# A gated DeltaNet stage whose matrix engine order is written by the program

## The chip, the cores and the metric

One core of one Trainium2 chip runs the kernel. The metric is device time in microseconds (us) from one run of the whole kernel. The instruction streams are PE (TensorE matmul), with PEld for its weight loads, DVE (VectorE), ACT (ScalarE), POOL (GpSimd), and SP, which issues all DMA transfers from one queue of instructions. Each engine starts its instructions in the order of its own stream.

## The reference

One inference step of a two-layer trunk for 512 prompt tokens and 8 sample tokens (T = 520), model width 1024, all in f32:

```python
for i in range(2):
    x = x + (gdn_mixer, dsw_mixer)[i](rmsnorm(x))
    x = x + square(relu(rmsnorm(x) @ w_up)) @ w_down
# gdn_mixer: 8 q/k heads of 128, 16 value heads of 128
proj = x @ w_in                               # q | k | v | z | b | a
q, k, v = silu(causal_conv4(proj[:3]))        # q, k: L2 norm per head
t_inv = inverse(I + strict(beta * (k @ k.T) * decay))     # per chunk
v_new = t_inv @ (v * beta) - t_inv @ (k * beta * exp(gc)) @ S
o = (q * exp(gc)) @ S + ((q @ k.T) * decay) @ v_new
S = S * exp(gc_last) + (k * exp(gc_last - gc)).T @ v_new  # next chunk
out = (rmsnorm(o) * silu(z)) @ w_out
```

The sample tokens take one step of the same recurrence, each from its own stored state S0 (16 heads of 8 x 128 x 128). The mixer of the second layer is a windowed attention. The change is inside the first mixer.

## The kernel before

The stages follow one another: gdn, mlp0, dsw, mlp1. Every product with a weight is made of three reduced-precision products (lines L165 to L167; a weight tile `raw` is split on ACT into `whi` and on DVE into `wlo`; tiles `mm` hold the results, 260 tokens at a time). One weight tile of 128 columns is 48 such matmuls.

The gdn stage works on eight pairs p = 0..7: one q/k head and its two value heads, in four chunks of 128 tokens, so eight units of 128 x 128 a pair. For each pair:

- `key`, `query`, `values`: projections, convolution, SiLU; PE transposes (`kqt`, `vtr`).
- `decay`: the DMA `ET <- Dg` (L595) brings cumulated log-decays over all partitions; DVE subtracts (L596), ACT takes absolute value and exponential (L597, L598); PE makes `kk` (L611) and DVE makes `E` from `kk` and `ET` (L603).
- `invert`: the 32 x 32 diagonal blocks of `E` go to DRAM (tile `D1`, L629) and come back spread over the partitions (`Ft`, L632); POOL substitutes in 31 steps of a multiply and an add (L638, L641; the buffer is a part of the tile `held`); the result goes to DRAM (`D2`, L642) and comes back as `Uf`, also a part of `held` (L646).
- `attend` (L618, POOL L619) turns `ET` into the attention matrix; `merge` (L653 to L683) joins inverted blocks by DVE transposes and small matmuls (`px`, `pu`).
- `scan`: for each chunk in turn the products `pk` (with the state `S`), `pv`, `pS` and `po`, with DVE, ACT and PE taking turns (`R` L712, `S` L724, `osb` L738 and L739).
- `sample`: loads the two `S0` tiles (L792, in `states`), products `sks` (L816), a transpose `sut` (L826), and the updated state by ACT and POOL (L837, L838) back to DRAM (L839).
- `gates`, `out`: the z projection; DVE scales `osb` (L862), PE transposes it (`otr`, L867), DVE gates it, and the split operands `onh` and `onl` go into the output projection, whose results DVE adds to x (L892).

A scheduler orders each engine's stream from the program order and priorities: the functions marked `urgent` get a priority of 2000. `states` of a pair stands at the pair's head in the program, ahead of `invert` of the next pair, and its DMAs keep program order:

```python
for p in range(QK_HEADS):
    A = pairs[p]
    A.states()
    A.values()
    if p < last:
        pairs[p + 1].key()
        pairs[p + 1].decay()
        pairs[p + 1].invert()
```

Of the kernel before, what the change touches and what calls it, by code (L numbers as in the profile page):

```python
# [38 lines left out]

KEEP = 104  # L40
# [9 lines left out]

class Common:
# [10 lines left out]
        # what lives as long as the kernel: the residual stream and constants, and the split operand  # L62
# [25 lines left out]
    def kept_rows(self):  # L88
        """The cached rows that stay in the sample's k/v buffers, a piece of them at each step."""
# [44 lines left out]
    def weights(self, cols, nk=KT):  # L134
        """cols: DRAM [nk * 128, n] pieces; gives each 128 columns in parts for the products."""
# [21 lines left out]
    def proj(self, w, mov, evac, m=P, halves=(0, 1)):  # L157
        nc = self.nc
        nk = len(mov)
        for hf in halves:  # L160
# [7 lines left out]
            evac(ps[:m], hf, s)  # L168
# [4 lines left out]
    def split_x(self, gain, k, hf, x=None):  # L173
        """The moving operand of the next projection, x * gain, as a rule not normalized yet."""
        nc = self.nc
        x = self.x if x is None else x
        s = slice(hf * H, hf * H + H)
        nc.scalar.activation(self.xh[:, k, s], x[:, k, s], AF.Copy, scale=gain[:, k : k + 1])  # L178
        nc.vector.scalar_tensor_tensor(  # L179
            self.xl[:, k, s], x[:, k, s], gain[:, k : k + 1], self.xh[:, k, s].bitcast(F32), ALU.mult, ALU.subtract  # L180
        )
# [14 lines left out]
    def mean_sq(self, acc):  # L196
        """1 / (mean square + eps) by token: [128, 5], the last column for the sample tokens."""
# [13 lines left out]
    def rsqrt(self, pool, x, eng, tag):  # L211
        """1 / sqrt(x) for positive x [128, n], by Newton's iteration from an estimate made of its bits."""
# [12 lines left out]
    def bcast(self, pool, r, tag="bc"):  # L225
        """A figure by token, [128, 5], over all partitions: [128, T]."""
# [21 lines left out]
    # the tensor engine's clock goes up with use: let it run while the rows come in  # L248
# [94 lines left out]
# before the scan of pair p: the output projection of some pairs, from one tile of x to another  # L343
OUTP = {p: [((p - 2,), 0, 8)] for p in range(2, 8)}
OUTP[8] = [((6,), 0, 8), ((7,), 0, 8)]
EARLY = (7,)
# [9 lines left out]
def gdn(K, l, rms, gain, done):  # L356
    """Gated DeltaNet, one pair of value heads (those of one q/k head) after the other, in chunks
    of 128 tokens. The first projections go without 1 / rms, which their result gets; meanwhile
    the moving operand is normalized for the rest."""
# [6 lines left out]
    with ExitStack() as ctx:  # L366
# [3 lines left out]
        xn = cp.tile([P, KT * T], F32, name="xn").rearrange("p (k t) -> p k t", k=KT)  # L370
        for k in range(KT):
            nc.gpsimd.tensor_tensor(xn[:, k], K.x[:, k], rb, ALU.mult)
# [19 lines left out]
        # eyeU[q4 * 32 + r, m, j] = (j == 4 * m + q4)  # L392
# [4 lines left out]
        # ---- beta and the log-decay, token-major  # L397
# [8 lines left out]
        # silu(x) = x/2 (1 + tanh(x/2)): the halves go to the weights, exactly  # L406
# [4 lines left out]
        # ---- the sample group's convolution history, feature-major: hist[p, f, b * 3 + j]  # L411
# [47 lines left out]
        # cumulated in each chunk; gc, its last, and their exponentials  # L459
# [7 lines left out]
        # gc as rows, in DRAM: a pair reads its own over all partitions  # L467
# [9 lines left out]
        # the sample tokens' beta and exp(g), over all partitions: [128, 2, 16, 8]  # L477
# [17 lines left out]
        # ---- buffers whose zero parts are set once  # L495
# [4 lines left out]
        def row(name):  # L500
            return K.tile(gp, [P, T], F32, tag="row", name=name, bufs=8)

        raw = []

        def project(w, ft, dest=None):
# [12 lines left out]
            if len(raw) < RAW:  # L518
# [3 lines left out]
                if len(raw) == RAW:  # L522
                    for hf in range(2):
                        for k in range(KT):
                            K.split_x(gain, k, hf, xn)
# [870 lines left out]
```

## Time and profile before

| | |
|---|---|
| median of 3 runs | 2165.23 us (2164.26 to 2168.29) |
| profiled execution, span | 2168.5 us |
| gdn stage in it, from the span's start | about 806 us |
| mlp0, dsw, mlp1 | about 1362 us |
| PE busy, whole span | 1989.6 us (92%) |
| PE busy in the first 806 us | 655.12 us |
| granted PE clock, first 806 us and rest | 0.87 and 1.00 |

The span is the profiled execution's time; it lies 3.3 us over the median of the three runs. The stage boundary is where the first activity of the MLP (L322) appears, at 807.8 us, with the last addition of L892 at 804.9 us. A PE that is busy at a granted clock of 0.87 does 0.87 of the work that it would do at full clock, so busy time times granted clock is the work of a stretch at full clock.

### The profile page before, as it was taken

Reading aid. Unit: us, or ns where it says so; the run is one execution under the profiler, and the core shown is the slowest. Engines: PE = TensorE matmul, PEld = TensorE weight load, DVE = VectorE, ACT = ScalarE, POOL = GpSimd, SP = SyncE. Lnnn points to the kernel's source line nnn. Section 1 sums busy time; section 2 is a strip of 40 time slices with the busy share of each in tenths; the row PEclk is TensorE's granted clock in tenths of the full one; section 3 lists DMA queues with packets and bytes.
Section 4 is the critical chain, followed back from the end, with each engine's and each line's share of the span. In section 5 each row is a group of like instructions: output and inputs, shape, how many; then the busy total and the mean of one; then the engine's idle time right before and its main releaser. Section 6 shows DMA issues by size and latency. Waiting matters only on the chain. (4 is left out here: it accounts for less than half of the span.)

```text
span 2168.5 us, 41683 instructions
## 1 busy us (share of the span) xinstructions
PE 1989.6 (92%) x16361; PEld 1950.9 (90%) x16361; DVE 1349.5 (62%) x3332; ACT 899.4 (41%) x2416; POOL 535.6 (25%) x821
## 2 busy tenths in 40 slices
PE   7677889896969789999999999999999989999999
PEld 6677778896969679999999999999999989999998
DVE  6754856785766584544556467676766785544544
ACT  5434444444334353223244555555555444233231
POOL 4253264355253230000002133232332250000000
PEclk8889989988979889999999999999999999999999
DMA  5334554764655538666676675534445343333332
GB/s 145 68 71 114 149 157 127 223 181 128 204 150 158 168 96 303 228 238 242 232 248 227 221 242 141 140 108 123 120 128 137 97 115 88 89 98 89 94 92 79
DMA packets 416277, 328.54 MB, mean 152 GB/s; under 512 B 48408, under 2 KB 404568, under 8 KB 413896
## 3 DMA queue, kind: packets, MB, share of 16 engines
q1 hardware_dynamic: 416080, 325.88, 50.4%
q8 instruction: 128, 2.10, 0.4%
q14 instruction: 69, 0.57, 0.1%
HBM read 302.19 MB, written 132.83 MB: 201 GB/s over the span
## 5 line engine op out<-in xcount | busy, mean ns | idle before, releaser
L165 PE MATMUL mm<-split,whi 128*128 128x260 f32 (+1 forms) x2960 | 866.7, 293 | 3.8 <-ACT split L178 2.5
L167 PE MATMUL mm<-split,wlo 128*128 128x260 f32 (+1 forms) x2960 | 851.8, 288 | 9.4 <-DVE wlo L132 9.4
L166 PE MATMUL mm<-split,whi 128*128 128x260 f32 (+1 forms) x2960 | 851.8, 288 | 8.7 <-DVE split L179 8.6
L166 PEld LDWEIGHTS mm<-split,whi 128*128 128x128 f32 (+1 forms) x2960 | 567.1, 192 | 12.3 <-DVE split L179 10.5
L167 PEld LDWEIGHTS mm<-split,wlo 128*128 128x128 f32 (+1 forms) x2960 | 566.5, 191 | 11.8 <-DVE wlo L132 10.9
L165 PEld LDWEIGHTS mm<-split,whi 128*128 128x128 f32 (+1 forms) x2960 | 567.6, 192 | 7.2 <-ACT split L178 3.7
L132 DVE TENSOR_TENSOR wlo<-raw,whi 128x1024 fp32r<-128x1024 f32 (+1 forms) x273 | 341.0, 1249 | 195.3 <-ACT whi L131 177.7
L131 ACT CAST whi<-raw 128x1024 fp32r<-128x1024 f32 (+1 forms) x273 | 285.8, 1047 | 411.7 <-PE mm L166 396.1
L167 PE MATMUL mm<-hh,wlo 128*128 128x260 f32 x1024 | 288.8, 282 | 0.0
L166 PE MATMUL mm<-hl,whi 128*128 128x260 f32 x1024 | 288.8, 282 | 0.0
L165 PE MATMUL mm<-hh,whi 128*128 128x260 f32 x1024 | 288.1, 283 | 0.0
L167 PEld LDWEIGHTS mm<-hh,wlo 128*128 128x128 f32 x1024 | 193.0, 188 | 0.0
L166 PEld LDWEIGHTS mm<-hl,whi 128*128 128x128 f32 x1024 | 192.8, 188 | 0.0
L165 PEld LDWEIGHTS mm<-hh,whi 128*128 128x128 f32 x1024 | 192.3, 188 | 0.0
L335 DVE TENSOR_TENSOR t<-mm,bc 128x260 f32<-128x260 f32 x128 | 54.8, 428 | 153.0 <-PE mm L167 153.0
L191 POOL TENSOR_TENSOR acc<-acc,sq 128x260 f32<-128x260 f32 x42 | 37.8, 909 | 382.0 <-ACT sq L190 381.3
L638 POOL TENSOR_TENSOR fs<-Ft,held 128x60 f32<-128x60 f32 (+24 forms) x248 | 100.5, 405 | 89.2 <-DMA Ft<-D 58.7
L131 ACT CAST hh<-q 128x260 fp32r<-128x260 f32 x128 | 52.5, 410 | 122.1 <-DVE q L322 122.1
L165 PE MATMUL mm<-onh,whi 128*128 128x260 f32 x256 | 90.3, 356 | 13.0 <-DVE base L892 7.9
L530 DVE SCALAR_TENSOR_TENSOR conv<-pre,held,conv 128x512 f32<-128x512 f32 x96 | 77.6, 808 | 30.1 <-POOL pre L508 27.2
L641 POOL TENSOR_TENSOR held<-held,fs 128x60 f32<-128x60 f32 (+24 forms) x248 | 90.5, 365 | 18.5
L132 DVE TENSOR_TENSOR hl<-q,hh 128x260 fp32r<-128x260 f32 x128 | 54.9, 429 | 57.0 <-ACT hh L131 57.0
(374 smaller groups left out, 3319.4 us busy)
## 6 DMA issues: line engine op xcount, KB each, us to landing
out_dram<-in_cache_kv_w_dram SPq DMA_DIRECT2D x112, 832.0 KB
raw<-in_dsw_w_in_dram SPq DMA_DIRECT2D x72, 512.0 KB
raw<-in_mlp_w_up_dram SPq DMA_DIRECT2D x64, 512.0 KB
raw<-in_mlp_w_down_dram SPq DMA_DIRECT2D x64, 512.0 KB
raw<-in_gdn_w_in_dram SPq DMA_DIRECT2D x48, 512.0 KB
S<-in_state_gdn_dram SPq DMA_DIRECT2D x16, 512.0 KB
raw<-in_gdn_w_out_dram SPq DMA_DIRECT2D x16, 512.0 KB
ub<-Du SPq DMA_DIRECT2D x16, 512.0 KB
```

Source lines behind the costliest of these rows:

```text
L131: nc.scalar.copy(hi, src)
L132: nc.vector.tensor_tensor(lo, src, hi.bitcast(F32), ALU.subtract)
L165: nc.tensor.matmul(ps[:m], lhsT=w[0][:, k, :m], rhs=xh[:, s], start=k == 0, stop=False)
L166: nc.tensor.matmul(ps[:m], lhsT=w[0][:, k, :m], rhs=xl[:, s], start=False, stop=False)
L167: nc.tensor.matmul(ps[:m], lhsT=w[1][:, k, :m], rhs=xh[:, s], start=False, stop=k == nk - 1)
L191: nc.gpsimd.tensor_tensor(acc[:, s], acc[:, s], t, ALU.add)
L335: nc.vector.tensor_tensor(t, ps, r2[:, s], ALU.mult)
L530: nc.vector.scalar_tensor_tensor(a, pre[:, j : j + NP], convw[:, ft, j : j + 1], a, ALU.mult, ALU.add)
L638: nc.gpsimd.tensor_tensor(tmp[:, :m, :n], Ft[:, None, j + 1 :, j].to_broadcast([P, m, n]), Uo[:, :m, j : j + 1].to_broadcast([P, m, n]), A ...
L641: nc.gpsimd.tensor_tensor(Uo[:, :m, j + 1 :], Uo[:, :m, j + 1 :], tmp[:, :m, :n], ALU.add)
```

## The change

In the gdn stage the scheduler no longer orders PE: the program does (`manual_schedule` for PE alone; DVE, ACT, POOL and SP are still ordered by the scheduler). The string `ORDER` lists the projections: K, Q, V, Z of each pair, and O for the output projection, for pairs 0 and 1, 2 and 3, 4 and 5 in one product each, then 6, then 7. A projection is a generator that yields after each three matmuls; the pair's other steps (`key_chain`, `query_chain`, `value_chain`, `scan`, `sample`, `out`) are generators too, launched with a model wait and stepped between those threes by `Weave`. The first ready item of the list is taken; K and Q of pair p want scan p - 3 emitted, V scan p - 2, Z out p - 2. Other edits:

- `gap` (the DMA `ET <- Dg`, the subtraction and the exponentials) is emitted at the start of `key_chain`, once scan p - 2 is emitted.
- `states` is called when the sample chain starts (after query p and sample p - 1), and `S0` has 2 buffers in place of 4.
- `kd` (two DVE products a pair, L555) is gone. ACT copies `kt`, and scales `vd` in each chunk; `pS` is one product of 256 columns in place of two of 128.
- `E` has 3 buffers in place of 2, and `osb`, `X1`, `X2`, `T2` become parts of `E`; `R` and `vn` have 1 buffer in place of 2, the rows of the projections 6 in place of 8.
- The clearing of `pre` goes from POOL to DVE. The normalised x of the later projections, made by POOL in eight products, is made after the sixth projection in row buffers, and no longer ahead of the stage.

```diff
+class Weave:
+    def __init__(self):
+        self.t, self.chains, self.done = 0.0, [], set()
+    def launch(self, steps, name, after=0.0):
+        self.chains.append([self.t + after, steps, name])
+    def pump(self):
+        for c in list(self.chains):
+            while c in self.chains and c[0] <= self.t:
+                self.step(c)
+    def step(self, c):
+        took, wait = next(c[1], (0.0, None))
+        self.t += took
+        if wait is None:
+            self.chains.remove(c)
...
+    def dense(self, steps):
+        for took in steps:
+            self.t += took
+            self.pump()
...
+                if k == nk - 1:
+                    evac(ps[:m], hf, s)
+                yield 3 * MMT
...
+ORDER = "K0 Q0 V0 K1 Q1 Z0 K2 Q2 V1 Z1 K3 Q3 V2 O01 Z2 K4 Q4 V3 Z3 K5 Q5 V4 O23 Z4 K6 Q6 V5 Z5 K7 Q7 V6 Z6 V7 Z7 O45 O6 O7"
+CONV_T, INV_T, SCAN_T, OUT_T, LOAD_T = 8.0, 60.0, (2.2, 2.2, 2.2), 5.0, 8.0
...
+            nc.vector.memset(pre[:, 0:3], 0.0)
...
+                    for k in range(KT):
+                        xn = row("xn")
+                        nc.gpsimd.tensor_tensor(xn, K.x[:, k], rb, ALU.mult)
+                        for hf in range(2):
...
-                kd = self.kd = K.tile(gp, [P, C4, 2, P], F32, tag="kd", name="kd", bufs=2)
-                for v in range(2):
-                    nc.vector.tensor_tensor(kd[:, :, v], pst, egc[:, 2, :, 2 * p + v, None].to_broadcast([P, C4, P]), ALU.mult)
+                kt = self.kt = K.tile(gp, [P, C4, P], F32, tag="kt", name="kt", bufs=2)
+                nc.scalar.copy(kt, pst)
                 nc.vector.tensor_scalar(ss, ss, EPS, None, ALU.add)
...
+                if p > 1:
+                    yield from W.until(f"scan{p - 2}")
+                self.gap()
...
+                yield 0.5, 2.0
+                with tc.high_priority(PRIO):
+                    self.decay()
+                    self.invert()
+                yield 4 * FULL, INV_T
+                yield from self.merge()
...
+                ET = self.ET = K.tile(gp, [P, U, P], F32, tag="ET", name="ET", bufs=2)
+                E4 = ET.rearrange("p (c v) d -> p c v d", v=2)
+                nc.sync.dma_start(E4, Dg[None, :, hh, :].to_broadcast([P, C4, 2, P]))
+                nc.vector.tensor_tensor(E4, E4, gc[:, :, hh, None].to_broadcast([P, C4, 2, P]), ALU.subtract)
+                nc.scalar.activation(ET, ET, AF.Abs)
+                nc.scalar.activation(ET, ET, AF.Exp, scale=-1.0)
...
+                E = self.E = K.tile(gp, [P, U, P], F32, tag="E", name="E", bufs=3)
...
+                W.launch(self.scan(), f"scan{p}")
+                W.launch(self.sample(), f"sample{p}", CONV_T)
...
+                osb = self.osb = self.E
...
+                            nc.scalar.activation(vd[:, v], pv[:, v * P : (v + 1) * P], AF.Copy, scale=egc[:, 2, c, 2 * p + v : 2 * p + v + 1])
+                        vn = K.tile(gp, [P, 2, P], F32, tag="vn", name="vn", bufs=1)
+                        nc.scalar.copy(vn.rearrange("p v d -> p (v d)"), pv[:, :256])
...
+                        nc.tensor.matmul(pS[:, :256], lhsT=self.kt[:, c], rhs=vd.rearrange("p v d -> p (v d)"), start=True, stop=True)
...
+                            W.launch(self.out(i, c0, c1), f"out{p}.{i}" if c1 < C4 else f"out{p}", 6 * FULL + 2.0)
+                    yield 6 * FULL, SCAN_T[2]
...
-                    S0 = K.tile(gp, [P, NS, P], F32, tag="S0", name="S0", bufs=4)
+                    S0 = K.tile(gp, [P, NS, P], F32, tag="S0", name="S0", bufs=2)
...
+                yield from W.until(f"query{p}", *([f"sample{p - 1}"] if p else []))
+                self.states()
...
+                yield 0.0, LOAD_T
...
+                yield from W.until(f"gates{p}", f"sample{p}", *([f"out{p}.{i - 1}"] if i else []))
...
+                yield 0.0, OUT_T
...
+        def waits(name, p):
+            if name == "O":
+                return [f"out{q}" for q in p if q < last] + [f"out{last}.1"] * (last in p)
+            n, of = dict(K=(3, "scan"), Q=(3, "scan"), V=(2, "scan"), Z=(2, "out"))[name]
...
+        with tc.manual_schedule(engines={mybir.EngineType.PE}):
+            while todo:
+                ready = [x for x in todo if W.done.issuperset(waits(*x)) and (x[0] != "Q" or ("K", x[1]) not in todo)]
+                if not ready:
+                    W.need(*waits(*todo[0]))
+                    continue
+                todo.remove(ready[0])
+                name, p = ready[0]
+                A = pairs[p[0]]
+                W.dense(out_proj(p, 0, KT) if name == "O" else {"K": A.key, "Q": A.query, "V": A.values, "Z": A.gates}[name]())
+            assert not W.chains, W.chains
```

How it moves instructions. First place: SP around the `S0` loads of pair 2 (tiles 2630 and 2632 before, 3111 and 3113 after) and the inversion of pair 3 (`D1`, `Ft`, `D2`). `raw` are weight loads, `out_9` and `out_10` cache rows copied through, `Du` the sample's u. Before, the stream of SP reads:

```order
L792 DMA S0_2630<-in_state_gdn_dram 128x8x128
L146 DMA raw_4486<-in_gdn_w_in_dram 128x8x128
L98 DMA out_9_dram<-in_cache_kv_w128_dram 16x2944
L792 DMA S0_2632<-in_state_gdn_dram 128x8x128
L629 DMA D1_2911<-E_2892 32x8x32 x4
L146 DMA raw_4493<-in_gdn_w_in_dram 128x8x128
L98 DMA out_9_dram<-in_cache_kv_w128_dram 16x13312
L632 DMA Ft_2917<-D1_2911 128x1x1024
```

After, the same place reads:

```order
L702 DMA D1_3008<-E_2994 32x8x32 x4
L705 DMA Ft_3014<-D1_3008 128x1x1024
L190 DMA raw_3587<-in_gdn_w_out_dram 128x4x256
L142 DMA out_9_dram<-in_cache_kv_w128_dram 16x13312
L190 DMA raw_3668<-in_gdn_w_in_dram 128x8x128
L142 DMA out_9_dram<-in_cache_kv_w128_dram 16x2944
L715 DMA D2_3009<-held_261 4x256x32
L719 DMA held_261<-D2_3009 32x8x32
L895 DMA S0_3111<-in_state_gdn_dram 128x8x128
L895 DMA S0_3113<-in_state_gdn_dram 128x8x128
```

The loads stood ahead of `D1` of pair 3, and now stand behind its `D2`. The same holds for pair 4 (behind `D2` of pair 5); pair 7's loads stand behind `D2` of pair 7 and behind the stores of pair 6's states. Those of the other pairs stand behind no `D2` of a later pair.

Second place: SP, the `ET` load of a pair and the `D2` store of another inversion. Before, `ET` of pair 4 stands ahead of `D2` of pair 3:

```order
L146 DMA raw_4745<-in_gdn_w_in_dram 128x8x128
L98 DMA out_10_dram<-in_cache_kv_w512_dram 16x13312
L595 DMA ET_3945<-Dg_429 128x4x256
L747 DMA out_2_dram<-S_3419 128x2x128
L146 DMA raw_4893<-in_gdn_w_in_dram 128x8x128
L98 DMA out_10_dram<-in_cache_kv_w512_dram 16x13312
L642 DMA D2_2912<-held_270 4x256x32
```

After, `ET` of pair 3 stands behind `D2` of pair 2 (`raw` are weight loads, `out_2` the final state of a scan):

```order
L715 DMA D2_2364<-held_261 4x256x32
L635 DMA ET_2920<-Dg_420 128x4x256
L190 DMA raw_3496<-in_gdn_w_out_dram 128x4x256
L719 DMA held_261<-D2_2364 32x8x32 x3
L850 DMA out_2_dram<-S_2884 128x2x128
```

From pair 2 on, each `ET` load now stands behind the `D2` store of the pair before; before, those of pairs 3, 4, 5 and 7 stood ahead of it.

Third place: PE, the transposes `otr` of pair 1's output, the `kk` of pair 3 and the `sks` of pair 2. Before, `otr` stands 122 rows behind the last `po` of its scan:

```order
L165 MATMUL mm_3772<-split_70,whi_3694 128x260
L166 MATMUL mm_3772<-split_70,whi_3694 128x260
L167 MATMUL mm_3772<-split_70,wlo_3695 128x260
L165 MATMUL mm_3772<-split_70,whi_3694 128x260
L166 MATMUL mm_3772<-split_70,whi_3694 128x260
L867 MATMUL otr_2605<-base_69,osb_2284 128x128 x4
L867 MATMUL otr_2614<-base_69,osb_2284 128x128 x4
```

After, it stands 43 rows behind it, right after `kk` of pair 3:

```order
L685 MATMUL kk_2995<-kq_2277 128x128 x4
L663 MATMUL kqt_3085<-base_69,kq_2277 128x128 x4
L685 MATMUL kk_3098<-kq_2277 128x128 x4
L782 MATMUL vtr_3105<-base_69,conv_2852 128x128 x4
L214 MATMUL mm_2978<-split_70,whi_2861 128x260
L215 MATMUL mm_2978<-split_70,whi_2861 128x260
L216 MATMUL mm_2978<-split_70,wlo_2862 128x260
L982 MATMUL otr_3132<-base_69,E_1238 128x128 x4
L982 MATMUL otr_3140<-base_69,E_1238 128x128 x4
L214 MATMUL mm_2978<-split_70,whi_2861 128x260
L215 MATMUL mm_2978<-split_70,whi_2861 128x260
L216 MATMUL mm_2978<-split_70,wlo_2862 128x260
```

From this `kk` to the first `sks` of pair 2 there are 60 projection matmuls and 21 others in all (rows of equal products taken apart), and from the last `po` of scan 1 (ahead of them) 93 and 33. Before, `sks` of pair 2 stands some 180 rows behind `kk` of pair 3.

Fourth place: DVE around the scaling of a pair's output (L862 before, L975 after; `osb` is now `E`) and the subtraction in `ET` for the pair two later. Before, the last rows ahead of the scaling of pair 1's output are these (wide `base` rows are steps of a Newton iteration); the subtraction for pair 3 stands some 30 rows earlier:

```order
L758 SCALAR_TENSOR_TENSOR sz_3448<-zt_3558,mm_3533 128x260
L783 COPY base_69<-sst_3092 128x16
L785 COPY base_69<-sst_3092 128x8
L222 SCALAR_TENSOR_TENSOR base_69<-base_69 128x24
L220 TENSOR_TENSOR base_69<-base_69 128x24
L221 TENSOR_TENSOR base_69<-base_69 128x24
L222 SCALAR_TENSOR_TENSOR base_69<-base_69 128x24
L220 TENSOR_TENSOR base_69<-base_69 128x24
L221 TENSOR_TENSOR base_69<-base_69 128x24
L222 SCALAR_TENSOR_TENSOR base_69<-base_69 128x24
L862 TENSOR_TENSOR osb_2284<-osb_2284,base_69 128x1024
```

After, for pair 5's output (`E_5036`) with the subtraction for pair 7:

```order
L636 TENSOR_TENSOR ET_7020<-ET_7020,held_261 128x1024
L271 TENSOR_TENSOR base_69<-base_69 128x4
L272 TENSOR_TENSOR base_69<-base_69 128x24
L272 TENSOR_TENSOR base_69<-base_69 128x4
L273 SCALAR_TENSOR_TENSOR base_69<-base_69 128x24
L273 SCALAR_TENSOR_TENSOR base_69<-base_69 128x4
L975 TENSOR_TENSOR E_5036<-E_5036,base_69 128x1024
```

In both, the subtraction stands ahead of the scaling. After, `E` of the pair two later (L676) stands behind it again, 9 rows further here.

More of the change, by code (lines that the diff above doesn't have):

```diff
@@ L38, in urgent @@
     return g
+MMT, FULL = 0.12, 0.225
 KEEP = 104
@@ L48, with need, until @@
 PACE = dict(gdn=1, mlp0=1, dsw=1, mlp1=1)
+class Weave:
[12 more added lines that the diff above has]
+            self.chains.remove(c)
+            self.done.add(c[2])
+        else:
+            c[0] = max(c[0], self.t) + max(wait, 0.05)
+    def dense(self, steps):
+        for took in steps:
+            self.t += took
+            self.pump()
+    def need(self, *names):
+        while not self.done.issuperset(names):
+            c = min(self.chains, key=lambda c: c[0])
+            self.t = max(self.t, c[0])
+            self.step(c)
+    def until(self, *names):
+        while not self.done.issuperset(names):
+            yield 0.0, 0.3
 class Common:
@@ L157, in proj, with proj_steps @@
     def proj(self, w, mov, evac, m=P, halves=(0, 1)):
+        for _ in self.proj_steps(w, mov, evac, m, halves):
+            pass
+    def proj_steps(self, w, mov, evac, m=P, halves=(0, 1)):
         nc = self.nc
@@ L515, in ev @@
                     nc.scalar.copy(news[:, ft, :], ps[:, H - NS :])
-            K.proj(w, mov, ev)
+            yield from K.proj_steps(w, mov, ev)
             if len(raw) < RAW:
@@ L532, in project @@
             nc.scalar.activation(t, a, AF.Tanh)
-            dest = a if dest is None else dest
-            nc.vector.scalar_tensor_tensor(dest, t, 1.0, a, ALU.add, ALU.mult)
-            return dest
+            if not out:
+                out.append(a)
+            nc.vector.scalar_tensor_tensor(out[0], t, 1.0, a, ALU.add, ALU.mult)
         class Pair:
@@ new lines, in merge @@
+                yield 1.7, 2.0
+                with tc.high_priority(PRIO):
+                    pus = {o: K.bank("pu", t).rearrange("p (u j) -> p u j", j=32) for o, t in ((0, "misc"), (64, "misc"))}
+                    for o in (0, 64):
+                        for u in range(U):
+                            t0 = T64[0:32, u, 0:32] if o == 0 else T2[:, u]
+                            nc.tensor.matmul(pus[o][o : o + 32, u], lhsT=t0, rhs=X1[o][:, u], start=True, stop=True)
+                        nc.scalar.copy(Uf[o : o + 32, :, o + 32 : o + 64], pus[o][o : o + 32, :U])
+                    for u in range(U):
+                        nc.tensor.matmul(pus[0][32:64, u], lhsT=X1[0][:, u], rhs=T64[0:32, u, 0:32], start=True, stop=True)
+                    nc.scalar.copy(T64[32:64, :, 0:32], pus[0][32:64, :U])
@@ new lines, in merge @@
+                yield 1.7, 2.5
+                with tc.high_priority(PRIO):
+                    px = K.bank("px2")
+                    pxt = px.rearrange("p (u j) -> p u j", j=64)
+                    for u in range(U):
+                        nc.tensor.matmul(pxt[0:64, u], lhsT=E[64:128, u, 0:64], rhs=Uf[64:128, u, 64:128], start=True, stop=True)
+                    nc.scalar.copy(X2, pxt[0:64])
+                yield 1.0, 2.0
+                with tc.high_priority(PRIO):
+                    pu = K.bank("pu2")
+                    put = pu.rearrange("p (u j) -> p u j", j=64)
+                    for u in range(U):
+                        nc.tensor.matmul(put[0:64, u], lhsT=T64[:, u], rhs=X2[:, u], start=True, stop=True)
+                    nc.scalar.copy(Uf[0:64, :, 64:128], put[0:64])
@@ L698, in scan @@
             def scan(self):
-                p, hh, kq, vt, col, Uf = self.p, self.hh, self.kq, self.vt, self.col, self.Uf
+                p = self.p
+                yield from W.until(*([f"scan{p - 1}"] if p else []), f"key{p}", f"query{p}", f"value{p}.0", f"value{p}.1")
+                hh, kq, vt, col, Uf = self.hh, self.kq, self.vt, self.col, self.Uf
                 S = None
-                oss = self.oss
-                osb = self.osb = K.tile(gp, [P, U, P], F32, tag="osb", name="osb")
+                oss, cuts = self.oss, LASTC if p == last else ((0, C4),)
@@ L742, in scan @@
-                    for v in range(2):
-                        u = 2 * c + v
-                        junk = K.tile(gp, [P, P], F32, tag="junk", name="junk", bufs=2)
-                        nc.scalar.activation(junk, osb[:, u], AF.Square, accum_out=oss[:, u : u + 1])
+                        with tc.high_priority(PRIO):
+                            Sf = S.rearrange("p v d -> p (v d)")
+                            pk = K.bank("pk", "scan", 256)
+                            nc.tensor.matmul(pk[:, :256], lhsT=kq[:, 0, cs], rhs=Sf, start=True, stop=True)
+                            r = K.tile(gp, [P, 2, P], F32, tag="R", name="R", bufs=1)
+                            for v in range(2):
+                                nc.vector.scalar_tensor_tensor(r[:, v], pk[:, v * P : (v + 1) * P], col[:, 2, c, v : v + 1], vt[:, c, v], ALU.mult, ALU.add)
@@ L888, in out_proj @@
                     for halves in ((0,), (1,)) if end else ((0, 1),):
+                        if halves == (1,):
+                            W.need(f"out{last}")
                         for k, w in ws:
@@ L894, in ev @@
                                     done(k, hf)
-                            K.proj(w, [m for p in ps for m in omov[p]], ev, halves=halves)
+                            yield from K.proj_steps(w, [m for p in ps for m in omov[p]], ev, halves=halves)
                     ws = []
```

273 lines of the change are left out of this document (116 added, 157 removed).

## The prediction

> **What bounds the kernel now.** I read the page's head, then the stretches of time before and after the end of the gdn stage, to see what the rest of the kernel can contribute.
>
> ```profile
> span 2168.5 us, 41683 instructions
> 0.00:806.00 806.00, 655.12 (x5267) 626.80 (x5268) 546.02 (x1546) 339.21 (x977) 329.69 (x662) 0.87 0.51 144
> 806.00:2168.00 1362.00, 1334.48 (x11097) 1324.14 (x11095) 803.48 (x1787) 560.22 (x1440) 205.92 (x159) 1.00 0.51 156
> 20.00:240.00 220.00, 164.22 (x1330) 154.84 (x1328) 145.90 (x405) 92.86 (x253) 85.46 (x181) 0.87 0.37 92
> 240.00:806.00 566.00, 475.74 (x3847) 457.81 (x3848) 393.73 (x1117) 234.11 (x700) 237.86 (x461) 0.87 0.56 161
> 774.00:806.00 32.00, 21.82 (x147) 20.09 (x146) 30.95 (x88) 18.18 (x51) 15.57 (x16) 0.84 0.34 102
> 850.00:950.00 100.00, 100.00 (x838) 100.00 (x837) 14.90 (x35) 6.49 (x17) 1.00 0.69 239
> ```
>
> The columns are the stretch, its length, busy time (and instructions) of PE, PEld, DVE, ACT, POOL, then PE's granted clock. After 806 us PE is full at clock 1.00, and the change does not touch that part. In the stage no engine is full: DVE is busy 546 of 806 us, PE 655. PE's work there at full clock is busy time times clock: 164.22 x 0.87 = 143 us in 20 to 240, and 475.74 x 0.87 = 414 in 240 to 806. So 77 us are lost in the first stretch and 566 - 414 = 152 in the second, to idleness and to the slow clock together. The second stretch starts where scan 1 starts. At full clock one projection matmul takes 100/838 = 0.119 us. What PE waits for, and what the SP queue waits for, in 20 to 806:
>
> ```profile
> PE sut L826 <- DVE base L819: 34.5, 5, 13.2
> PE px L660 <- DMA held<-D: 21.4, 3, 11.3
> PE pv L715 <- DVE R L712: 13.7, 4, 8.9
> SPq L642 <- POOL held L526: 37.9, 2, 19.6
> SPq L642 <- POOL held L641: 37.6, 4, 15.0
> SPq L146 <- DVE wlo L132: 111.1, 16, 18.3
> ```
>
> So no single wait bounds the stage: PE's losses are chains of small latencies, the longest the inversion. The SP rows matter most for what follows: SP stands still at the `D2` store (L642) until POOL has finished. One pair's inversion in order of time:
>
> ```profile
> 409.56 2.15 DVE L603 SCALAR_TENSOR_TENSOR E<-kk,base,ET 128x128 f32<-128x128 f32 x8
> 411.74 1.81 SPq L629 DMA_DIRECT2D D<-E  x4
> 428.28 1.21 POOL L638 TENSOR_TENSOR fs<-Ft,held 128x31 f32<-128x31 f32 x1 [7.33 <-DMA Ft<-D]
> 456.22 0.61 SPq L642 DMA_DIRECT2D D<-held  x1
> ```
>
> From the end of `E` (411.7) to the `D2` store there are 44.5 us.
>
> **The change, part by part.** The work of PE hardly changes: `pS` streams the same 256 columns. I therefore keep 414 us for the second stretch and 77 us lost for the first, and put the whole change into one question: how much is lost after scan 1's start, against 152 us.
>
> *Gain.* The new order has 309 to 417 projection matmuls (37 to 50 us) and 60 to 133 small ones between a pair's `kk` and its `px`. So the wait on the inversion, and those inside scans that other work now separates, have cover: all of the 152 us is up for removal, except what follows.
>
> *Sample states (S0).* The price of a load is in these rows: the first `sks` starts 5.7 us after its load is issued, and waits for it.
>
> ```profile
> 747.55 2.21 SPq L792 DMA_DIRECT2D S<-in_state_gdn_dram  x2
> 753.25 1.95 PE L816 MATMUL sks<-base,S 128*128 128x2 f32 x16 [1.57 <-DMA S<-in_state_gdn_dram]
> ```
>
> For pairs 2 and 4 the loads now stand behind `D2` of the next pair's inversion, so they issue no earlier than 44.5 us after that pair's `E`, and arrive at about 50. PE reaches `sks` 60 projection matmuls and 21 small ones after `kk`: 60 x 0.119 = 7.2 us, and some 2.5 us at the rate of the eight `kk` in the row of the next fence, so 10 us. PE's order is fixed, so nothing passes the waiting `sks`. Pair 7 waits likewise on its own inversion, but reaches `sks` 303 projection matmuls (36 us) and 89 others after `kk`, about 50 us; with the stores of pair 6 ahead in the queue I take 10 us, between 0 and 20.
>
> *ET and the output transposes.* `ET` is loaded only after the last `po` of scan p - 2, as before; the question is what PE does meanwhile.
>
> ```profile
> 437.27 0.37 SPq L595 DMA_DIRECT2D ET<-Dg  x1
> 446.52 1.26 DVE L596 TENSOR_TENSOR ET<-ET,held 128x1024 f32<-128x1024 f32 x1 [4.47 <-DMA ET<-Dg]
> 437.03 1.06 PE L735 MATMUL po<-S,kq 128*128 128x256 f32 x2
> 458.30 2.61 DVE L862 TENSOR_TENSOR osb<-osb,base 128x1024 f32<-128x1024 f32 x1
> 461.35 0.82 PE L867 MATMUL otr<-base,osb 128*128 128x128 f32 x6
> 409.95 1.05 PE L611 MATMUL kk<-kq 128*128 128x128 f32 x8
> ```
>
> Before, `otr` runs 24 us after the last `po`, with other work between. Now PE is there after 6 to 9 us, while DVE has the subtraction, then rows of the Newton iteration and of convolutions, then the scaling ahead of it. From the last `po`: 0.2 to issue, 9.25 to land, 1.26 to subtract, 2 to 9 for the rows between (about 0.17 us a small one and 0.8 us a convolution step, by their counts for each pair), 1.2 to 2.6 to scale. That is 14 to 20 us, and PE waits 9, 12, 10, 5 and 6 us for the outputs of pairs 0, 2, 3, 4 and 5. Pair 1 is worse: `ET` of pair 3 stands behind `D2` of pair 2. `E` of pair 2 ends some 21 us after scan 0, `D2` issues 44.5 later, at 65; PE is through scan 1 after 35 us of work (198 projection matmuls, 24 us, and 51 others, mostly the scan's larger products), the wait of 9 and some slow clock, at 48. `ET` is thus 17 us late and `otr` ready 38 us after the last `po`: a wait of 29.
>
> With these the `sks` waits follow. Pair 4: `E` of pair 5 at 21 after scan 3, loads arrive at 21 + 44.5 + 5.7 = 71; PE has done 18 (84 projection matmuls, 10 us, and 81 others) and waited 10, and waits 43 more. Pair 2: `E` of pair 3 at 42, loads arrive at 92; PE is there at 15 + 29 = 44, and waits 48. Sum of `sks` 48 + 43 + 10 = 101 (bounds 70 and 120: the bare 44.5 + 5.7 less 15, twice, and all of it), sum of `otr` 71 (bounds 36, with six waits of 6 us if DVE's rows between are done early, and 95).
>
> *Slow clock.* A hole is followed by a slow stretch:
>
> ```profile
> 181.90:191.10 9.20, 0.30 (x4) 0.09 (x2) 1.74 (x5) 0.00 (x0) 0.56 (x4) 0.75 0.26 47
> 191.10:210.00 18.90, 18.90 (x135) 18.80 (x136) 8.58 (x19) 8.47 (x24) 1.01 (x2) 0.85 0.54 178
> 530.50:542.10 11.60, 0.32 (x5) 0.14 (x3) 3.71 (x12) 4.08 (x9) 0.00 (x0) 0.68 0.56 72
> 542.10:560.00 17.90, 17.90 (x174) 16.88 (x175) 13.51 (x35) 4.08 (x11) 4.91 (x2) 0.73 0.33 109
> ```
>
> The 18.9 us after the first lose 0.15 x 18.9 = 2.8 us, the 17.9 after the second 0.27 x 17.9 = 4.8. Nine waits (six `otr`, three `sks`) at 3.8 make 34, between 25 and 43. The Trainium skill ("TensorE: Matmul & The Clock Gate", Part 1: The HAM clock gate) says that an idle window of about 3.4 us halves the rate and about 3.4 us of busy time restores it; the trace agrees on the fall and shows a longer recovery. By the page a hole would cost 1.7 us, nine 15, and the estimate would come out 19 us lower; I go by the rows.
>
> *Tail.* After the last `po` the stage loses 32 - 21.82 x 0.84 = 14 us; I keep it (5 to 25).
>
> *The rest* I take as nothing:
>
> ```profile
> L555 DVE TENSOR_TENSOR kd<-kqt,held x16: 674/680/693, 65.2 to 659.1; 128x512 f32<-128x512 f32 x16
> DVE conv L530 <- POOL pre L508: 27.2, 9, 5.4
> ```
>
> `kd` takes 16 x 0.68 = 11 us off DVE and clearing on DVE ends DVE's 27 us of waiting on POOL; the ACT copies in their place fall into ACT's 58% of idle time. All three lie under PE's own waits; where that cover goes, as in a scan whose steps become bare, `vd` ahead of `vn` adds some 0.4 us to each of 32 chunks, 13 us at most. Normalising x later puts eight POOL products beside the first inversion, on which the first transposes, and behind them weight splits on DVE, then wait. Before scan 1 I therefore allow from 10 us gained to 15 lost, and take 0.
>
> *Sum.* 101 + 71 + 34 + 14 = 220 lost after scan 1's start, against 152: 68 us more. The profiled execution would take 2168.5 + 68 = 2236; it lies 3.3 over the median, so I forecast 2233. Low ends together, 70 + 36 + 25 + 5 - 10 = 126, would be 26 us faster (2139); high ends, 120 + 95 + 43 + 25 + 15 = 298, 146 slower (2311).
>
> **Rivals.** *Faster: the state loads do not hold PE.* SP is not in fact behind at `D2` when the loads are due. Then the 101 goes, `ET` of pair 3 is on time, and what is left is 36 + 6 x 3.8 + 14 = 73 us: 79 less than before, 2086. For it speaks that SP waited at L642 at most 19.6 us at a time before. Against it: before, ten other transfers stood between `D1` and `D2` of pair 3, five stand there now, and POOL's chain takes its 44.5 us whenever SP comes; the loads would have to issue within 5 us of `E`. The inversion would have to be nine times shorter.
>
> *About the same: the long waits absorb the short ones.* While PE stands at `sks`, DVE and ACT finish everything queued, and the later `otr` waits shrink to 6 us each; the `sks` waits come out at their low end. 70 + 36 + 34 + 14 = 154: 2167. For it: DVE is busy 394 of 566 us, with room. Against: `ET` cannot be loaded before the last `po`, which comes after the wait.
>
> *Slower still: weights.* A `D2` store that holds SP also holds weight loads; between `D1` and `D2` of pairs 3 and 5 only two and one weight loads stand. SP already waits 111 us on `wlo` to have free buffers, so it runs close to its consumers. If PE runs dry for 8 us after each of eight inversions, 64 us come on top: 2297. Against: PE stands still during the two worst of them.
>
> **Chances.** The forecast's case 0.52 (its own range 2195 to 2275), the faster rival 0.18, the same 0.14, weights 0.16. What the runs of this kernel can tell from no change is about 0.2%, 4 us. The middle rival falls on both sides: 0.03 faster, 0.06 same, 0.05 slower. So faster 0.21, same 0.06, slower 0.73. The range is 2130 to 2300: it leaves out the faster rival and little else.
>
> **What would show it.** In the profile after, the longest PE waits should be `sks` on the DMA of S, two or three times of 40 us or more, and `otr` on DVE's scaling, six times, with pair 1's the longest; the SP queue's wait at the `D2` store should grow from 20 to 40 us at a time; waits of `px` and `pv` should nearly vanish. The stage should end near 874 us, and the stretch after it take 1362 us as before. I am wrong if `sks` waits under 10 us in sum, which is the faster rival, or if `mm` waits on `wlo` by tens of us, which is the weights. If PE's waits are as forecast and the stage is still short, the 152 us were removed more fully elsewhere than I allow, above all before scan 1.

## The result, and the profile after

| | before | changed |
|---|---|---|
| median, 4 runs each | 2166.76 us (2164.26 to 2172.53) | 2295.24 us (2290.26 to 2299.51) |
| profiled execution, span | 2168.5 us | 2291.7 us |
| first MLP activity (end of the gdn stage) | 807.8 us | 927.5 us |

The ratio is 1.0586, with a 95% interval of 1.0564 to 1.0608: 128 us slower. The forecast of 2233 had the sign and lay 62 us low; the time is just inside the range.

The head of the page after and its stretches (length, then busy time and instructions of PE, PEld, DVE, ACT and POOL, then PE's granted clock); scan 1 starts at 237 us:

```profile
span 2291.7 us, 41582 instructions
20.00:237.00 217.00, 156.37 (x1162) 145.61 (x1159) 122.44 (x363) 87.98 (x244) 88.13 (x167) 0.78 0.36 92
237.00:927.00 690.00, 496.40 (x3955) 478.18 (x3954) 377.02 (x1121) 264.57 (x779) 210.50 (x446) 0.82 0.45 132
930.00:2290.00 1360.00, 1334.83 (x11064) 1324.36 (x11062) 795.45 (x1783) 558.99 (x1435) 206.01 (x158) 1.00 0.51 156
897.60:927.00 29.40, 22.69 (x152) 21.71 (x150) 25.13 (x62) 18.41 (x49) 12.35 (x14) 0.83 0.16 45
```

The rest of the kernel takes 1364 us where it took 1361; nearly the whole loss is in the stage. A finer account splits the stage from 20 us to its end into three parts: PE idle (length less busy time), slow clock (half of the time in which a matmul ran while the clock's records grant half speed), and the rest, PE's work at full clock. For before: 146 idle, 74 slow, 568 work. After: 254, 90 and 563. So of 120 us, 108 are idle PE. This replaces busy time times mean clock, by which work was reckoned before the result. That product also charges work for half speed granted while PE stood idle: after scan 1 it gives 496.40 x 0.82 = 407 us of work, and the account gives 437. Some of PE's waits, 20 to 940 us (total, times, longest); of those left out the longest are 19.3 us of `vtr` behind `conv` and 15.3 of `mm` behind `split`, mostly ahead of scan 1:

```profile
PE sks L923 <- DMA S<-in_state_gdn_dram: 68.4, 3, 35.6
PE kk L685 <- ACT junk L666: 18.2, 3, 8.2
PE pv L809 <- DVE R L804: 18.2, 4, 14.5
PE pk L801 <- DVE S L823: 15.2, 2, 14.2
PE otr L982 <- DVE base L988: 14.0, 2, 7.8
PE pk L801 <- DVE base L870: 11.9, 1, 11.9
PE kk L685 <- DVE sz L860: 11.0, 1, 11.0
PE kk L685 <- DVE E L838: 8.7, 1, 8.7
PE otr L982 <- DVE E L975: 8.3, 2, 7.4
PE vtr L782 <- DVE E L676: 7.5, 2, 6.7
```

Three groups can be read from it. `sks` waits for the state loads, 68 us. The rows of `kk` and `otr`, and `vtr` behind `E`, make 68 us. And `pk` and `pv`, inside scans, wait 45 us for small DVE steps. Of the first group, one hole in order of time:

```profile
318.90 2.62 SPq L702 DMA_DIRECT2D D<-E  x4
333.04 0.59 SPq L142 DMA_DIRECT2D out_dram<-in_cache_kv_w_dram  x1
356.84 0.60 SPq L715 DMA_DIRECT2D D<-held  x1
361.59 0.34 SPq L719 DMA_DIRECT2D held<-D  x1
361.97 1.08 SPq L895 DMA_DIRECT2D S<-in_state_gdn_dram  x2
366.33 1.83 PE L923 MATMUL sks<-base,S 128*128 128x2 f32 x8 [35.63 <-DMA S<-in_state_gdn_dram]
```

SP stands at `D2` from 333.6 us to 356.84, then waits for it to land and loads part of `Uf`, and only then issues the states. The second hole, 32.17 us before the `sks` at 592.02, has the same shape (`D2` issues at 582.65). For the second group, the place that the forecast named, pair 3's `ET` behind pair 2's `D2`:

```profile
295.08 0.69 DVE L783 TENSOR_TENSOR vt<-vtr,base 128x512 f32<-128x512 f32 x1 [10.11 <-POOL held L714]
296.25 2.04 PE L685 MATMUL kk<-kq 128*128 128x128 f32 x8 [8.74 <-DVE E L838]
295.08 0.61 SPq L715 DMA_DIRECT2D D<-held  x1
295.79 2.18 SPq L635 DMA_DIRECT2D ET<-Dg  x1
307.71 1.23 DVE L636 TENSOR_TENSOR ET<-ET,held 128x1024 f32<-128x1024 f32 x1 [10.86 <-DMA ET<-Dg]
310.15 2.07 PE L685 MATMUL kk<-kq 128*128 128x128 f32 x8 [11.01 <-DVE sz L860]
```

DVE stands 10.86 us at the subtraction, and what PE waits for is a small DVE step queued behind it. Not all of this group is `ET`. The first two rows show PE waiting 8.7 us at `kk` while DVE stands at `vt` until POOL's last inversion step, and 6.2 us at the last `otr` (909.92) come after the last `ET`; that leaves some 53 of the 68. The third group was not in the forecast. DVE's own waits, 20 to 940, and the three places:

```profile
DVE E L731 <- DMA held<-D: 83.3, 3, 35.8
DVE held L729 <- DMA held<-D: 51.1, 4, 19.0
DVE ET L636 <- DMA ET<-Dg: 40.5, 8, 10.9
498.95 0.43 DVE L729 STREAM_TRANSPOSE held<-held 32x256 f32<-32x256 f32 x1 [15.61 <-DMA held<-D]
502.24 1.19 PE L801 MATMUL pk<-S,kq 128*128 128x256 f32 x2 [11.92 <-DVE base L870]
722.07 0.43 DVE L729 STREAM_TRANSPOSE held<-held 32x256 f32<-32x256 f32 x1 [13.96 <-DMA held<-D]
726.77 1.22 PE L809 MATMUL pv<-R,held 128*128 128x128 f32 x4 [14.50 <-DVE R L804]
806.23 0.43 DVE L729 STREAM_TRANSPOSE held<-held 32x256 f32<-32x256 f32 x1 [19.03 <-DMA held<-D]
808.47 1.22 PE L801 MATMUL pk<-S,kq 128*128 128x256 f32 x2 [14.15 <-DVE S L823]
```

`merge` opens with DVE transposes of `Uf` (L729 to L731). PE's order puts merge late; DVE's order, which the scheduler still makes, puts these transposes early, ahead of steps of the scan that runs meanwhile. DVE stands until the inversion has landed, and the scan, which does not need it, stands too: 11.9 + 14.5 + 14.2 = 41 us.

### The profile page after: what moved, and what is told of

Same layout as the page of the kernel before. It is cut to its first block, busy times and chain, and to the rows that moved or that the text cites. A ratio compares the mean times of both kernels' runs of the same rounds, so it can differ in the third digit from the quotient of the medians.

```text
span 2291.7 us, 41582 instructions
## 1 busy us (share of the span) xinstructions
PE 2005.1 (87%) x16297; PEld 1964.3 (86%) x16297; DVE 1304.8 (57%) x3300; ACT 926.7 (40%) x2488; POOL 511.0 (22%) x789
## 4 chain that ended last, share of the span: by engine, by line
PE 60%; DMA 12%; DVE 11%; POOL 9%; ACT 4%; issue 3%; SPq 1%; DVEq 0%; POOLq 0%; ACTq 0%
PE mm L214 17%; PE mm L216 17%; PE mm L215 17%; DMA Ft<-D 4%; POOL fs L711 4%; POOL held L714 3%; DMA ET<-Dg 3%; DVE wlo L176 2%; DMA D<-held 1%; DVE conv L582 1%; DVE split L230 1%; PE po L1305 1%; PE tr L1158 1%; PE sks L923 1%; ACT whi L175 1%
## 5 line engine op out<-in xcount | busy, mean ns | idle before, releaser
L214 PEld LDWEIGHTS mm<-split,whi 128*128 128x128 f32 (+1 forms) x2960 | 572.7, 193 | 32.3 <-ACT split L229 16.9
L711 POOL TENSOR_TENSOR fs<-Ft,held 128x60 f32<-128x60 f32 (+24 forms) x248 | 88.9, 358 | 105.8 <-DMA Ft<-D 87.5
L175 ACT CAST hh<-q 128x260 fp32r<-128x260 f32 x128 | 52.5, 410 | 122.3 <-DVE q L373 122.3
L923 PEld LDWEIGHTS sks<-base,S 128*128 128x128 f32 x256 | 40.0, 244 | 69.2 <-issue 68.1
L923 PE MATMUL sks<-base,S 128*128 128x2 f32 x256 | 39.4, 285 | 68.4 <-DMA S<-in_state_gdn_dram 68.4
L582 DVE SCALAR_TENSOR_TENSOR conv<-pre,held,conv 128x512 f32<-128x512 f32 x96 | 85.8, 894 | 1.0 <-ACT conv L580 0.4
```

What stands on the lines that cost most here:

```text
L175: nc.scalar.copy(hi, src)
L214: nc.tensor.matmul(ps[:m], lhsT=w[0][:, k, :m], rhs=xh[:, s], start=k == 0, stop=False)
L582: nc.vector.scalar_tensor_tensor(a, pre[:, j : j + NP], convw[:, ft, j : j + 1], a, ALU.mult, ALU.add)
L711: nc.gpsimd.tensor_tensor(tmp[:, :m, :n], Ft[:, None, j + 1 :, j].to_broadcast([P, m, n]), Uo[:, :m, j : j + 1].to_broadcast([P, m, n]), A ...
L923: nc.tensor.matmul(pst[:, b], lhsT=S0[:, b], rhs=kqs[:, b], start=True, stop=True)
```

## The experiments

By the traces' matmuls, in order and by name, the first six keep PE's order but for at most 21 of 16,297; what moves is the order of the other engines, and who issues a DMA. "Before", run again beside each of them, took 2168.8 to 2172.3 us (medians), and each ratio is against that. The account of idle, slow and work is of the profiled execution, from 20 us to the first MLP activity.

| run | median, us | against before (95%) | idle | slow | work |
|---|---|---|---|---|---|
| before | 2166.8 | | 146 | 74 | 568 |
| changed | 2295.2 | 1.0586 (1.0564 to 1.0608) | 254 | 90 | 563 |
| states early | 2262.9 | 1.0439 (1.0415 to 1.0463) | 224 | 90 | 565 |
| transposes in order | 2282.5 | 1.0518 (1.0495 to 1.0542) | 245 | 87 | 564 |
| both | 2229.3 | 1.0275 (1.0250 to 1.0300) | 195 | 82 | 564 |
| both, ET early | 2239.3 | 1.0326 (1.0306 to 1.0347) | 198 | 93 | 563 |
| D2 on POOL alone | 2277.1 | 1.0500 (1.0469 to 1.0531) | 228 | 104 | 562 |
| both, D2 on POOL | 2205.6 | 1.0171 (1.0145 to 1.0196) | 181 | 76 | 564 |
| that, ET early and pinned | 2192.9 | 1.0119 (1.0083 to 1.0156) | 154 | 100 | 562 |
| that, `kd` on DVE again | 2191.7 | 1.0113 (1.0097 to 1.0130) | 157 | 88 | 564 |

**States early.** Where PE waited longest, the loads go back to where they stood.

```diff
-S0 = K.tile(gp, [P, NS, P], F32, tag="S0", name="S0", bufs=2)
+S0 = K.tile(gp, [P, NS, P], F32, tag="S0", name="S0", bufs=4)
 def values(self):
     p = self.p
+    self.states()      # no longer in sample()
```

> The changed kernel with the sample states loaded as before the change: four S0 buffers, and the two loads at the head of values, which stands ahead of the next pair's inversion in the program. Theory A (SP's queue): PE's waits for the DMA of S, 68 us in two long holes, and the slow clock behind them, 4 us each, go: 60 to 80 us less than the changed kernel, 2215 to 2235 us. Rival B (one latency loop from E over the inversion to the scan paces the stage, and a wait that is taken away comes back at px or in DVE's transposes): under 20 us less, over 2275.

32 us less, between the two. The rows show both halves: of the `sks` waits one of 24.9 us is left (68.4 before), since pair 5's loads now stand behind a `D2`; and DVE's transposes hold more.

```profile
PE sks L923 <- DMA S<-in_state_gdn_dram: 24.9, 1, 24.9
PE pk L802 <- DVE S L828: 27.5, 2, 15.5
DVE held L729 <- DMA held<-D: 114.9, 8, 27.8
```

So a part of what the long wait had covered came back at DVE.

**Transposes in order.** The three transposes stay behind what was written before them for DVE.

```diff
-nc.vector.transpose(T64[0:32, :, 0:32], Uf[0:32, :, 0:32])
+tc.keep_in_program_order(nc.vector.transpose(T64[0:32, :, 0:32], Uf[0:32, :, 0:32]))
 # and the two after it
```

> The changed kernel with the three DVE transposes that open merge kept in program order on DVE, so that they no longer stand ahead of scan steps which PE reaches first. Theory C (DVE stands still on the inversion's result while the scan of the pair before needs it): the three waits of pv and pk, 41 us, and the slow clock behind them go: 35 to 55 us less than the changed kernel, 2240 to 2260, and DVE's waits for that DMA (134 us) shrink to under 90. Rival B: the waits move to px, which then follows later: under 15 us less, over 2280.

13 us less: far under theory C, and the size that the rival gave, though not for its reason, since PE does not wait at `px`. The waits of `pv` and `pk` are gone (2.3 us of `pv` left), and DVE no longer waits for `Uf`; but `sks` waits 79.2 us (68.4) and `ET` holds DVE 66.7 us (40.5).

```profile
PE pv L809 <- DVE R L804: 2.3, 2, 1.3
PE sks L923 <- DMA S<-in_state_gdn_dram: 79.2, 4, 35.7
DVE ET L636 <- DMA ET<-Dg: 66.7, 8, 19.9
```

Alone, either edit frees PE for the next wait in the queue.

**Both.**

> Both edits: states early and transposes in program order. If A and C both hold and do not cover each other: 95 to 135 us less than the changed kernel, 2160 to 2200, about the kernel before. Rival B: over 2250.

66 us less, more than 32 + 13: the two waits had covered for one another. That is half of the 128, and under the forecast. What is left is the second group, `ET` (61.6 us of DVE's time), and pair 5's `sks` (23.6).

```profile
PE sks L923 <- DMA S<-in_state_gdn_dram: 23.6, 1, 23.6
DVE ET L636 <- DMA ET<-Dg: 61.6, 8, 16.8
```

**ET early, not pinned.** Two `S0` buffers, a third `ET` buffer, and `gap` written ahead of the wait for scan p - 2.

```diff
-ET = self.ET = K.tile(gp, [P, U, P], F32, tag="ET", name="ET", bufs=2)
+ET = self.ET = K.tile(gp, [P, U, P], F32, tag="ET", name="ET", bufs=3)
+self.gap()
 if p > 1:
     yield from W.until(f"scan{p - 2}")
-self.gap()
```

> Both edits, with two S0 buffers for space, and a third ET buffer, with the load of ET and its exponentials emitted ahead of the wait for scan p-2. Theory D (ET behind the last po, and behind D2 in the queue, makes DVE stand and PE wait at kk and otr, about 60 us): a further 30 to 70 us less than with the two edits, 2100 to 2165. Rival E (what is left is slow clock and the scans' own steps): within 15 us of the run with both edits.

10 us more than with both, within what rival E allowed. The load may go earlier, but the scheduler also moves the subtraction forward on DVE, which then stands longer: 70.5 us, the longest 23.4. For pair 7 DVE stands from 560.3 us, and the load issues only at 562.5. PE's wait at `kk` grows to 25.4 at a time. The two `S0` buffers in place of four are a second difference: `sks` waits 30.3 us, from 23.6, so the 10 us are not `ET`'s alone.

**D2 on POOL.** POOL, which makes `D2`, issues its store and the loads of `Uf`; SP no longer stands there.

```diff
-nc.sync.dma_start(D2.rearrange("b u (m q) j -> q (b u) m j", q=4), Uo)
+nc.gpsimd.dma_start(D2.rearrange("b u (m q) j -> q (b u) m j", q=4), Uo)
-nc.sync.dma_start(Uf[s, :, s], D2[b].rearrange("u m j -> m u j"))
+nc.gpsimd.dma_start(Uf[s, :, s], D2[b].rearrange("u m j -> m u j"))
```

> The changed kernel with the D2 stores and the loads of Uf issued by POOL, which has just made D2, and no longer by SP. All else as in the changed kernel, the late S0 loads and DVE's order among it. Theory A (SP stands at D2 with the S0 and ET loads queued behind it): PE's waits for the DMA of S fall from 68 us to under 15, ET of pair 3 issues right after the last po; 40 to 75 us less than the changed kernel, 2220 to 2255 us. Rival (S0 loads late by their own emission, or waits handed on to DVE's transposes as in the run with states early, which gave 32): 20 to 40 less, 2255 to 2275.

With PE's order and the late state loads untouched:

```profile
PE sks L923 <- DMA S<-in_state_gdn_dram: 12.6, 2, 7.3
PE pv L809 <- DVE R L804: 42.2, 5, 19.5
DVE held L729 <- DMA held<-D: 102.6, 8, 19.9
```

The wait for S falls from 68.4 to 12.6 us, as the queue theory says; that shows the place. The time falls by only 18, under both figures: the transposes take the gap, and `pv` waits 42 us.

> States early, transposes in program order, and D2 and Uf on POOL's queue. Theory A: the one sks wait left in the run with both edits (24 us) goes and ET loads are no longer delayed by SP: 25 to 50 us under that run (2229), 2180 to 2205. Rival F (POOL's issue of these DMAs lengthens the inversion, or the rest is DVE's wait for ET alone): within 12 us of 2229.

With both earlier edits the same step gives 24 us more (2229.3 to 2205.6), at the edge of what theory A said. `sks` no longer stands among PE's waits for a DMA. SP still reaches the `ET` loads late, though: three are issued 9.7, 14.0 and 13.2 us after the last `po` that they wait for, and DVE waits 68.9 us for `ET`. SP now stands ahead of them at the sample's steps, which wait for POOL:

```profile
SPq L949 <- POOL S L948: 50.6, 6, 21.8
SPq L944 <- POOL S L948: 42.8, 4, 21.0
```

**ET early and pinned.** The subtraction is written 12 us of model time after the load and kept in program order on DVE, with three `ET` buffers and two of `S0`.

```diff
+self.gap()             # the DMA alone
+yield 0.0, 12.0
+self.gap2()            # keep_in_program_order(subtract), abs, exp
 if p > 1:
     yield from W.until(f"scan{p - 2}")
-self.gap()
```

> As the run before (two S0 buffers for space), with a third ET buffer, ET's load emitted ahead of the wait for scan p-2 and its subtraction kept in program order on DVE 12 us of model time later. Theory D (DVE standing at the subtraction until ET has landed, 53 us in the run with both edits, makes PE wait at kk and otr): 20 to 50 us under the run before. Rival E: within 10 us of it, or slower, as the first early ET was.

13 us less, to 2192.9, between the two figures (four runs from 2187.7 to 2203.6, against 2203.1 to 2209.4). This edit also moves 444 matmuls of PE's order. The wait itself went:

```profile
DVE ET L642 <- DMA ET<-Dg: 0.9, 1, 0.9
PE pS L826 <- ACT vd L820: 26.1, 4, 18.5
20.00:836.00 816.00, 661.97 (x5119) 631.40 (x5119) 510.47 (x1488) 354.16 (x1025) 344.99 (x652) 0.83 0.49 137
```

DVE now waits 0.9 us for `ET`, from 68.9 in the run before, and idle PE falls to 816 - 662 = 154 us, near the 146 of before. But 100 us go to the slow clock, from 76. Part of that is this one execution: the profiled run took 2203.6 us, 11 over the median. With `kd` on DVE again, profiled at its median and no different in time, the account has 157 idle and 88 slow.

**Two pairs at a time.**

```diff
-... O01 ... O23 ... O45 O6 O7
+... O0 O1 ... O2 O3 ... O4 O5 O6 O7
```

> The changed kernel with the output projection of one pair at a time (O0 O1 in place of O01, and so on); nothing else changed. If two pairs at a time matter: fewer additions on DVE (64 in place of 128) were a gain and the time rises by 5 to 20 us. If the loss is all queue order: within 10 us of the changed kernel, 2285 to 2305.

2294.5 us, ratio 1.0586 (1.0565 to 1.0608): no difference. This half of the change is worth nothing either way.

**Three edits on the best run so far.** The normalised x made ahead of the stage again:

> The run with ET early and pinned (2193 us), with the normalised x made by POOL ahead of the stage in its own tile, as before the change. Theory G (the start is dearer than forecast: POOL's eight products stand inside the first inversion, PE waits 13 us for splits at 81 us and then runs 37 us at half clock): the first inversion from E to D2 shortens from about 50 us, PE does more before scan 1, and the time falls by 12 to 30 us, to 2163 to 2181. Rival H (PE then waits for the first inversion instead, as before the change): within 8 us of 2193.

2201.0 us, ratio 1.0156 (1.0129 to 1.0184): no gain, 8 us more, the edge of the rival's figure. A hole of 12.6 us at 81 us (PE on splits) gave way to one of 16.9 at 94 us, which the trace puts down to no releaser. `kd` on DVE again:

> The run with ET early and pinned (2193 us), with kd made by DVE ahead of the scan as before the change, so pS no longer waits for two ACT products in each chunk. Theory I (these lie on the scan's path: PE waits 26 us at pS for vd, one wait of 18): 8 to 25 us less. Rival J (the 18 us are ACT standing behind something else and come back elsewhere; DVE has 11 us more): within 8 us.

2191.7 us, ratio 1.0113 (1.0097 to 1.0130): no difference. `pS` no longer waits for `vd`, and `pv` waits 21.8 us for `R`, once 16.8. Longer scan steps:

> The run with ET early and pinned (2193 us), with the model wait of a scan step raised from 2.2 to 4 us: about 33 matmuls between two steps of a scan in place of 21. Theory K (the steps' true latency is over 2.2 us, so PE stalls a little at many of them and its clock falls; 100 us were lost to the slow clock in that run): 5 to 20 us less. Rival L (longer scans delay the E of the pair two later and leave less for later): 5 to 30 us more.

2209.5 us, ratio 1.0196 (1.0173 to 1.0218), 17 us slower: the rival's size. Its reason is not shown. The waits at `pS` shrink to 6.8 us and idle PE is about the same (152 us), but the stage ends at 837.5 us in the profile, against 836.2 in the profile of ET early and pinned (the execution of 2203.6 us) and 828.6 in that with `kd` on DVE, so the profiles do not place the 17 us.

**D2 on POOL in the kernel before.** The last run asks whether the same step helps where the scheduler orders PE.

> The kernel before the change, with the D2 stores and the Uf loads issued by POOL and no longer by SP; the scheduler orders PE and DVE anew around it. Theory A carried over (SP stands 76 us at D2 there too, with weight, ET and state loads behind it, and Uf waits for its turn): 5 to 20 us less than before, 2147 to 2162. Rival M (in the scheduler's own order other work covers SP's wait, which is why the kernel before does not show it at PE): within 4 us, or slower by what POOL's issuing costs.

2193.0 us, ratio 1.0103 (1.0073 to 1.0133): 21 us slower. The profile shows the price of the step, which the changed order had mostly hidden (there `px` waited 10.7 us, from 1.2):

```profile
L642 POOL DMA_DIRECT2D D<-held x8: 2077/2077/2263, 129.8 to 725.2; - x8
L646 POOL DMA_DIRECT2D held<-D x32: 582/582/610, 142.3 to 736.1; - x32
PE px L660 <- DMA held<-D: 52.5, 7, 17.6
DVE held L653 <- DMA held<-D: 65.2, 7, 13.3
```

Issued by POOL, the `D2` store takes 2.08 us of POOL, where SP took 0.61, and from the last step of the first inversion to its first transpose there are 14.9 us (129.5 to 144.4) where there were 7.6 (130.9 to 138.5). In the kernel before, `px` waits for that: 52.5 us, from 21.4. The stage ends 12.5 us later (820.3); the scheduler ordered all engines anew around the step, so how much of the 21 us is the step's own is not isolated. In the changed order the inversion is mostly covered, and freeing SP was worth 24.

## Why the prediction was right in sign and short in size

- *State loads behind D2: right place, 101 forecast, 68 measured.* Two holes of 35.6 and 32.2 us and none for pair 7, where 48, 43 and 10 were forecast. The smaller part of the gap is the loads: they let `sks` start 47.4 and 45.9 us after `E`, not 50. `D2` came earlier than 44.5 us after `E` (37.9 in the first hole, 318.9 to 356.8), but SP then waited for it to land before it issued the loads. The larger part is PE, which stood at `sks` 11.8 and 13.8 us after `E`, not 2 and 7: it waited 6.7 us at `vtr` for `E` on the way to the first, and ran at half speed on the way to both (until 325.0, and from 546.9 to 557.1 us).
- *ET and otr: 71 forecast, 68 measured.* Pair 3's `ET` issued right behind `D2` as said. PE waited for it at `kk` and `vtr` as much as at `otr`: 38 us of the 68 are at `kk`. DVE standing at the subtraction holds everything behind it, which the forecast had put on `otr` alone: `otr` waits four times for more than 0.5 us, not six. That the sums agree is partly luck, since 15 of the 68 are the waits at `vt` and in the tail that are not `ET`'s.
- *The gain that failed: all 152 us "up for removal, except what follows".* The step was wrong in leaving out DVE's order around `merge`. I counted PE work between `kk` and `px` as cover for the inversion; it covers PE, but DVE takes up the result early in its own stream, and 41 us of scan waits followed. Of the waits in the scan, `pv` did not nearly vanish, while `px` did. SP's longest wait at `D2` is 23.6 us, from 19.6, and not the 40 that was given as a sign.
- *Slow clock: 34 forecast, 60 measured after scan 1*, from the clock's records. I priced the nine holes that I had listed; there were more, and some of the slow time, as at 215 us, stands after no hole at all.
- *Work and start: taken as unchanged.* Scan 1 starts at 237 us as forecast (240 before), but by then PE has done 126 us of work in place of 147 by the finer account, and 437 were left after it, where I had put 414. That is 23 us. By the same account before had 421 after its scan 1, so 16 of them are work that came later and 7 the coarse product of busy time and mean clock.
- *Tail: 14 forecast*, 29.4 - 22.69 x 0.83 = 11 measured.

After scan 1 the forecast had 414 + 220 = 634 us, and there were 690. Of the 56 us between, 41 are the transposes, 26 the clock and 23 the work; the terms of the states and of ET take 36 back, and the tail's 14 go, since what it cost is already in the `otr` waits and the slow clock. The 16 left are small waits that no term names.

Of the rivals, the "faster" one was wrong as argued: SP does stand at `D2`. The "same" one was wrong about the size, but its mechanism is real: taking one wait away lengthened another in each run that did so alone (states early, transposes in order, D2 on POOL). The weight rival was not seen; PE's `mm` waits 0.2 us for `wlo` in the stage and 11.7 in the whole span.

What stays open: the best version is still 1.1% behind before. By its account (`kd` on DVE again) PE idles 11 us more, loses 14 more to the slow clock and has 3 less work; what in PE's order costs the clock was not isolated. No version beat the kernel before.

## What to carry to other kernels

When the program fixes one engine's order, the orders of the others, still made from a model's times, must agree with it: one early instruction in an in-order stream (a store on the DMA queue, a transpose on DVE) stops everything behind it. So read a new order stream by stream, and for each instruction that waits for a long result ask what is queued behind it. Where waits cover one another, a run that removes one of them shows little; remove them together before judging: here 32 and 13 us apart were 66 us together.

## What the runs showed of the hardware

A DMA of the same bytes issued by POOL held its engine 2.08 us where SP took 0.61, and POOL then waited 55.2 us in eight times for the store to land, 6.9 us each, where SP's loads behind the same store had waited 18.9 us in eight times. SP had other transfers to issue meanwhile, so the longest waits compare better: 10.2 us and 4.1. Moving a transfer to the engine that makes its data frees a queue, but it lengthened the transfer's own path by some 7 us in the first inversion.

And the granted clock was down for 13.7 us from 215.8 us although PE was busy nearly all that time, with 141 matmuls in 22 us, mostly small ones of scan 0 and merge:

```profile
215.00:237.00 22.00, 20.08 (x141) 16.62 (x137) 4.82 (x17) 10.31 (x37) 4.62 (x3) 0.61 0.30 98
210.00:215.80 5.80, 5.80 (x74) 5.69 (x74) 3.07 (x13) 5.53 (x18) 0.00 (x0) 1.00 0.37 104
215.80:229.50 13.70, 13.56 (x104) 11.17 (x103) 2.42 (x8) 6.44 (x22) 3.70 (x2) 0.50 0.13 48
```

By the rule of the Trainium skill weighed in the prediction ("TensorE: Matmul & The Clock Gate", Part 1: The HAM clock gate), a busy PE should have its clock back after about 3.4 us; these rows do not agree.

The clock fell with no hole ahead of it: PE is busy throughout 210.0 to 215.8. The projection matmuls end at 210.2 us, and none runs in the half-speed stretch. Its slowness is real: four `pv` products took 0.69 us at 211.9 and 1.22 at 224.0. In the run with ET early and pinned the clock is halved for 27.3 us from 195.5 us, with 1.5 us of idle PE and again no projection matmul. In both places the clock fell while PE ran small products alone; no run isolates that as the cause.
